# A hybrid decoder trunk: two pairs of column groups in each feed-forward stage become 2x2 block products with seven multiplications

## The chip, the core and the metric

One core of one Trainium2 chip runs the whole kernel in one launch. The metric is the device time of one execution in microseconds (us), lower is better. Before the change the three runs shown took 1042.58, 1043.15 and 1047.03 us, median 1043.15 us.

## What is computed

Two layers, and in each of them three stages on x of 256 tokens by 1024 channels, float32:

```
x += 1/2 * rmsnorm(swiglu(rmsnorm(x, g1)), post1)     # feed-forward stage 1
x +=       rmsnorm(hybrid_mix(rmsnorm(x, gm)), postm) # token mixing
x += 1/2 * rmsnorm(swiglu(rmsnorm(x, g2)), post2)     # feed-forward stage 2
swiglu(h) = (silu(h @ w_gate) * (h @ w_up)) @ w_down  # 1024 -> 2816 -> 1024
```

`hybrid_mix` projects to 2432 columns, runs four head groups side by side (a short gated convolution, a gated MLP over chunks, an RWKV-7 recurrence in chunk form, a convolution module) and projects back to 1024. The change touches the feed-forward stages; in the mixing it touches only how buffers are laid out.

## The kernel before, in words

The tokens are two tiles of 128 rows (b = 0, 1). A feed-forward stage walks through 11 column groups of 256 hidden channels. For a group i there are three weight blocks in memory: two for the gate and up columns side by side (1024 rows by 512 columns, in two row halves of 512 rows each) and one for the down projection. Each block is loaded as two tiles of 128 partitions x 1024 elements (512 KB), so a group has six loads.

`split` (line 124) makes one such load usable for TensorE. It loads the tile into one of four staging buffers (`raw`, line 127, issued on SyncE's queue), ScalarE rounds it to the float32r type (`whi`, line 135), and VectorE subtracts that from the staged tile (`wlo`, line 136). The tags `w` and `w2` give 14 and 10 buffers, so 12 pairs of parts exist at a time. `mm3` (lines 142 to 145) multiplies with three matmuls: high by high, high by low, low by high. The activations are split in the same way (`xh`, `xl`, lines 181 and 182).

`GU(b, i)` (line 243) is the gate/up product of one token tile with one group: 8 row blocks x 3 = 24 matmuls of 128x512 into one PSUM bank, then silu on ScalarE and the gating on VectorE; both read the bank and both scale by `r`, the norm's factor of each token. `TR(b, i)` (line 257) transposes the 256 gated channels on TensorE and splits the result (`hh`, `hl`). `DN(b, i)` (line 268) is the down product: 12 matmuls into two banks that accumulate over the whole stage. From group 2 on the loop (line 305) traces, for each group i: the loads and splits of group i, GU(0, i), TR(1, i-1), the loads of the down block i-1, DN(0, i-1), TR(0, i), GU(1, i), DN(1, i-1). That makes 24 + 12 + 24 + 12 = 72 matmuls of 128x512 and two calls of TR for each turn of the loop.

No order is written out by hand there. A scheduler that runs when the program is built walks through the traced instructions by priority, lets one go ahead of an earlier one when its operands and a free buffer are there by its own estimate of times, and so fixes the order of each engine's queue. On the chip each engine then takes its queue strictly in that order, and waits at the head when an operand is late. Calls marked `keep_in_program_order` or `later` are pinned.

PSUM has eight banks: four for the down sums (`acc`), two for products (`mm`) and two for transposes (`tp`). In SBUF the work pools are `c1` (10 buffers of 256 columns), `c2` (4 of 512), `f1` (8 of 256) and `f2` (4 of 512). The prenorm (lines 160 to 200) transposes x into `xg`, multiplies by the gain and splits it; `mix` (line 325) has its own single buffers for `lora`, `sgw`, `sgln`, `DC`, `caT`, `zc` and `pc0`, `pc1`.

Of the kernel before, what the change touches and what calls it, by code (L numbers as in the profile page):

```python
# [41 lines left out]
C1 = 10  # L42
# [6 lines left out]
def trunk_kernel(ctx: ExitStack, tc: tile.TileContext, a, out):  # L49
# [5 lines left out]
    act = ctx.enter_context(tc.tile_pool(name="act", bufs=1))  # L55
    work = ctx.enter_context(tc.tile_pool(name="work", bufs=2))
# [103 lines left out]
    def prenorm_steps(l, b, gname):  # L160
        xh = act.tile([P, KT, P], F32R, name=f"xh{b}")
        xl = act.tile([P, KT, P], F32R, name=f"xl{b}")
# [3 lines left out]
        def turn(h, pin=False):  # L166
# [6 lines left out]
            xg[h] = work.tile([P, 4, P], F32, name="xg", tag="f2", bufs=F2)  # L173
# [5 lines left out]
        def parts(h):  # L179
            sl = slice(4 * h, 4 * h + 4)  # L180
            nc.scalar.copy(xh[:, sl, :], xg[h])
            nc.vector.tensor_tensor(out=xl[:, sl, :], in0=xg[h], in1=xh.bitcast(F32)[:, sl, :], op=ALU.subtract)

        def stats():
# [6 lines left out]
            return xh, xl, r[:, 0:1]  # L191
# [3 lines left out]
    def prenorm(l, b, gname, pin=False):  # L195
        turn, parts, stats = prenorm_steps(l, b, gname)
# [25 lines left out]
    def ffn(l, f, nxt, first):  # L222
# [20 lines left out]
        def GU(b, i, middle=None):  # L243
            xh, xl, r = X[b]
            pg = mm_bank("pgu")
            for k in range(KT):
                hi, lo = gu[i][k // 2]
                mm3(pg, xh[:, k, :], xl[:, k, :], hi, lo, (k % 2) * 512, 512, k == 0, k == KT - 1)
# [35 lines left out]

        prep_gu(0)
# [19 lines left out]
        for i in range(2, NG):  # L305
            if first and i == 3:
                late_constants()
            prep_gu(i)
            GU(0, i)
            TR(1, i - 1)  # L310
            prep_dn(i - 1)
            DN(0, i - 1)
            TR(0, i)
            GU(1, i)
            if i == NG - 1:
# [3 lines left out]
            DN(1, i - 1)  # L319
# [5 lines left out]
    def mix(l, nxt):  # L325
        gp = load_gp(3 * l + 1)
        X = nxt["X"]
        lora = act.tile([P, 768], F32, name="lora")
        later(lora, a["lora"][l])
        sgw = act.tile([P, 4, P], F32, name="sgw")  # L330
        later(sgw, a["sgw"][l])
        sgln = act.tile([P, 512], F32, name="sgln")
# [35 lines left out]
        def proj(g, b):  # L368
            n = GROUPS[g][1]
            xh, xl, r = X[b]  # L370
            pairs, kp = W[g]
            pg = mm_bank("pin")
            for k in range(KT):
                hi, lo = pairs[k // kp]
                mm3(pg[:, 0:n], xh[:, k, :], xl[:, k, :], hi, lo, (k % kp) * n, n, k == 0, k == KT - 1)
# [9 lines left out]
        pc = [act.tile([P, 11, P + 1], F32, name=f"pc{b}") for b in range(NB)]  # L385
# [3 lines left out]
        def c_in(b):  # L389
            r = X[b][2]  # L390
# [11 lines left out]
        def c_prep(b):  # L402
# [45 lines left out]
            # kappa, its squared norm  # L448
# [20 lines left out]
            # chunk operands  # L469
# [20 lines left out]
            # v with tokens on partitions, bonus  # L490
# [39 lines left out]
        DC = act.tile([P, 8, 32], F32, name="DC")  # L530
# [6 lines left out]
        def c_base():  # L537
            # the inverse of every 16x16 diagonal block, even and odd columns on a partition each
# [75 lines left out]
        def own(bank):  # L614
            # of the four heads' regions, the columns that are the head's own
# [92 lines left out]
        zT = act.tile([P, 2, 256 + 30], F32, name="zT")  # L708
        nc.gpsimd.memset(zT[:, :, 0:30], 0.0)
        ca_T = act.tile([P, 2, 256 + 2], F32, name="caT")  # L710
# [9 lines left out]
        def d_in(b):  # L720
            pg = proj(2, b)
            r = X[b][2]
# [12 lines left out]
        zc = act.tile([P, 2, 256], F32, name="zc")  # L735
# [30 lines left out]
        def a_in(b):  # L766
            r = X[b][2]
# [10 lines left out]
        def a_out(b):  # L778
            r = X[b][2]
# [19 lines left out]
        def b_in(b):  # L799
            r = X[b][2]  # L800
# [94 lines left out]
    turn, parts, stats = prenorm_steps(0, 0, "g1")  # L895
# [12 lines left out]
    def third_step():  # L908
        cur["X"][1] = prenorm(0, 1, "g1", True)

    for n, (kind, l, f, _) in enumerate(phases):
        nx = {"X": [None, None]}
        if n + 1 < len(phases):
            nl, ng = phases[n + 1][1], phases[n + 1][3]

            def start(b, nl=nl, ng=ng, nx=nx):
                nx["X"][b] = prenorm(nl, b, ng)
# [127 lines left out]
```

## Time and profile before

| | |
|---|---|
| runs, median | 1042.58 to 1047.03, 1043.15 us |
| profiled execution, its span | 1043.0 us |
| TensorE matmul | busy 98% of the span |
| VectorE / ScalarE / GpSimd | 64% / 51% / 7% |
| bytes moved | 177 MB, 170 GB/s on average |

The profiled execution gives its span, from the first to the last instruction; no other time is known for it, and its 1043.0 us lie 0.15 us below the median of the runs. The busy time of TensorE counts matmuls whose ends are modelled, so that neighbours overlap: a matmul shown with 0.39 us starts about 0.23 us after the one before it. What a matmul costs is therefore read from the distance between two starts, not from its duration.

### The profile page before, as it was taken

Reading aid. Unit: us, or ns where it says so; the run is one execution under the profiler, and the core shown is the slowest. Engines: PE = TensorE matmul, PEld = TensorE weight load, DVE = VectorE, ACT = ScalarE, POOL = GpSimd, SP = SyncE. Lnnn points to the kernel's source line nnn. Section 1 sums busy time; section 2 is a strip of 40 time slices with the busy share of each in tenths; the row PEclk is TensorE's granted clock in tenths of the full one; section 3 lists DMA queues with packets and bytes.
Section 4 is the critical chain, followed back from the end, with each engine's and each line's share of the span. In section 5 each row is a group of like instructions: output and inputs, shape, how many; then the busy total and the mean of one; then the engine's idle time right before and its main releaser. Section 6 shows DMA issues by size and latency. Waiting matters only on the chain.

```text
span 1043.0 us, 13547 instructions
## 1 busy us (share of the span) xinstructions
PE 1018.7 (98%) x4914; PEld 834.5 (80%) x4914; DVE 669.7 (64%) x1072; ACT 533.7 (51%) x848; POOL 69.5 (7%) x133
## 2 busy tenths in 40 slices
PE   7999999999999999999999999999999999999997
PEld 6888888888797788888887888888878887888885
DVE  6754645689998655464676454647999895645442
ACT  6653534468466545353555353536665674535331
POOL 1000000210012100000010000003000130000000
PEclk8999999999999999999999999999999999999999
DMA  7865546254044654555536555544432356555521
GB/s 274 299 206 187 189 174 209 95 174 149 18 159 163 224 202 163 200 176 188 185 139 230 194 181 182 192 153 146 167 107 79 104 205 239 174 189 187 176 81 40
DMA packets 50322, 177.23 MB, mean 170 GB/s; under 512 B 5840, under 2 KB 6352, under 8 KB 50256
## 3 DMA queue, kind: packets, MB, share of 16 engines
q1 hardware_dynamic: 49968, 175.86, 49.9%
q8 instruction: 38, 0.62, 0.2%
q10 hardware_dynamic: 288, 0.52, 0.1%
q14 instruction: 28, 0.23, 0.1%
HBM read 175.31 MB, written 1.05 MB: 169 GB/s over the span
## 4 chain that ended last, share of the span: by engine, by line
PE 87%; DVE 7%; DMA 2%; POOL 1%; issue 1%; ACT 1%; SPq 0%; DVEq 0%; POOLq 0%; ACTq 0%
PE pgu L144 15%; PE pgu L143 15%; PE pgu L145 15%; PE dn L143 8%; PE dn L144 8%; PE dn L145 8%; PE pin L144 3%; PE pin L145 3%; PE pin L143 3%; DMA raw<-in_ffn 2%; PE hTp L261 2%; PE zp L586 1%; PE xT L170 1%; PE wo L143 1%; PE wo L144 1%
## 5 line engine op out<-in xcount | busy, mean ns | idle before, releaser
L136 DVE TENSOR_TENSOR wlo<-raw,whi 128x1024 fp32r<-128x1024 f32 x324 | 393.3, 1218 | 123.7 <-ACT whi L135 109.0
L135 ACT CAST whi<-raw 128x1024 fp32r<-128x1024 f32 x324 | 338.0, 1047 | 154.1 <-DMA raw<-in_ffn 63.4
L143 PE MATMUL pgu<-whi,xh 128*128 128x512 f32 x704 | 280.4, 398 | 4.0 <-ACT whi L135 4.0
L144 PE MATMUL pgu<-wlo,xh 128*128 128x512 f32 x704 | 276.7, 393 | 0.5 <-DVE wlo L136 0.5
L145 PE MATMUL pgu<-whi,xl 128*128 128x512 f32 x704 | 276.0, 392 | 0.0
L143 PEld LDWEIGHTS pgu<-whi,xh 128*128 128x128 f32 x704 | 132.8, 189 | 31.7 <-ACT whi L135 4.3
L145 PEld LDWEIGHTS pgu<-whi,xl 128*128 128x128 f32 x704 | 132.8, 189 | 28.9
L144 PEld LDWEIGHTS pgu<-wlo,xh 128*128 128x128 f32 x704 | 132.9, 189 | 27.4 <-DVE wlo L136 1.0
L143 PE MATMUL dn<-whi,hh 128*128 128x512 f32 x352 | 143.1, 406 | 3.6 <-ACT hh L264 3.6
L144 PE MATMUL dn<-wlo,hh 128*128 128x512 f32 x352 | 139.7, 397 | 0.0
L145 PE MATMUL dn<-whi,hl 128*128 128x512 f32 x352 | 138.1, 394 | 0.0
L252 ACT ACTIVATE silu<-pgu,rpre 128x256 f32<-128x256 f32 x88 | 41.5, 472 | 153.2 <-PE pgu L145 153.2
L254 DVE SCALAR_TENSOR_TENSOR h<-pgu,rpre,silu 128x256 f32<-128x256 f32 x88 | 42.3, 481 | 114.8 <-ACT silu L252 114.5
L265 DVE TENSOR_TENSOR hl<-hTp,hh 128x256 fp32r<-128x256 f32 x88 | 36.8, 418 | 91.2 <-ACT hh L264 91.2
L264 ACT CAST hh<-hTp 128x256 fp32r<-128x256 f32 x88 | 32.4, 368 | 99.1 <-PE hTp L261 99.0
L143 PEld LDWEIGHTS dn<-whi,hh 128*128 128x128 f32 x352 | 66.2, 188 | 19.1 <-ACT hh L264 4.9
L145 PEld LDWEIGHTS dn<-whi,hl 128*128 128x128 f32 x352 | 66.0, 188 | 16.9 <-DVE hl L265 1.0
L144 PEld LDWEIGHTS dn<-wlo,hh 128*128 128x128 f32 x352 | 66.2, 188 | 13.5
L144 PE MATMUL pin<-wlo,xh 128*128 128x512 f32 (+2 forms) x192 | 70.7, 371 | 0.0
L145 PE MATMUL pin<-whi,xl 128*128 128x512 f32 (+2 forms) x192 | 70.5, 371 | 0.0
L143 PE MATMUL pin<-whi,xh 128*128 128x512 f32 (+2 forms) x192 | 70.5, 371 | 0.0
L745 DVE SCALAR_TENSOR_TENSOR zc<-zT,par,zc 128x256 f32<-128x256 f32 x120 | 49.8, 477 | 3.2 <-ACT zc L742 3.1
(212 smaller groups left out, 908.4 us busy)
## 6 DMA issues: line engine op xcount, KB each, us to landing
raw<-in_ffn SPq DMA_DIRECT2D x264, 512.0 KB, 4.5
raw<-in_wout SPq DMA_DIRECT2D x16, 512.0 KB, 3.6
raw<-in_win_z SPq DMA_DIRECT2D x8, 512.0 KB, 4.5
raw<-in_win_rk SPq DMA_DIRECT2D x8, 512.0 KB, 5.0
raw<-in_win_ca SPq DMA_DIRECT2D x8, 512.0 KB, 4.3
raw<-in_win_uv SPq DMA_DIRECT2D x8, 512.0 KB, 4.5
gp<-in_post_g SPq DMA_DIRECT2D x6, 512.0 KB, 4.6
raw<-in_win_vl SPq DMA_DIRECT2D x8, 384.0 KB, 3.0
```

What stands on the lines that cost most here:

```text
L135: i0 = nc.scalar.copy(hi[:, 0:n], raw[:, 0:n])
L136: i1 = nc.vector.tensor_tensor(out=lo[:, 0:n], in0=raw[:, 0:n], in1=hi.bitcast(F32)[:, 0:n], op=ALU.subtract)
L143: nc.tensor.matmul(dst, lhsT=sh, rhs=hi[:, c0:c0 + n], start=start, stop=False)
L144: nc.tensor.matmul(dst, lhsT=sh, rhs=lo[:, c0:c0 + n], start=False, stop=False)
L145: nc.tensor.matmul(dst, lhsT=sl, rhs=hi[:, c0:c0 + n], start=False, stop=stop)
L170: t = nc.tensor.transpose(tp[:, k * P:(k + 1) * P], x[b][:, kk * P:(kk + 1) * P], ident)
L252: nc.scalar.activation(out=s, in_=pg[:, 0:256], func=AF.Silu, scale=r)
L254: nc.vector.scalar_tensor_tensor(out=h, in0=pg[:, 256:512], scalar=r, in1=s, op0=ALU.mult, op1=ALU.mult)
L261: nc.tensor.transpose(tp[:, j * P:(j + 1) * P], h[:, j * P:(j + 1) * P], ident)
L264: nc.scalar.copy(hh, tp[:, 0:256])
L265: nc.vector.tensor_tensor(out=hl, in0=tp[:, 0:256], in1=hh.bitcast(F32), op=ALU.subtract)
L745: nc.vector.scalar_tensor_tensor(out=zc[:, j, :], in0=zT[:, j, k:k + 256], scalar=w, in1=zc[:, j, :], op0=ALU.mult, op1=ALU.add)
```

## The change

In each feed-forward stage the groups (4, 5) and (7, 8) are taken as pairs. With the two token tiles as block rows and the two halves of the 1024 input channels as blocks of the inner dimension, a pair is a 2x2 by 2x2 block product; each block product is 12 matmuls. It is computed with seven block products (the Winograd form of Strassen's scheme) where eight stood. The signs are put on the token side, so that all sums of weight blocks are plain additions:

```
s1 = x10 - x11    s2 = s1 - x00    s3 = x00 - x10    s4 = x01 + s2
T1 = Bi0 + Bm0    T2 = T1 + Bm1    T3 = Bm0 + Bm1    T4 = T2 + Bi1
```

Here xbh is token tile b, channel half h, and Bgh the gate/up block of group g (i is the first of the pair, m the second), row half h. T1, T2 and T4 are made in place, one after the other, in the two tiles `chain`; T3 is made in two staging buffers. Each addition is a DMA issued from GpSimd that adds the tile in HBM to the tile in SBUF (`accum_op=ALU.add`). Each of the seven weight operands is split into high and low parts.

For these sums the token factor `r` has to be in the operands, not behind the product: after group 2 `scaled(b)` transposes `r` on TensorE and multiplies it into the kept `xg`, and `put` splits the result; groups from 3 on use these tiles (`A`). `forms()` makes s1 to s4. All such operands, the activations of the mixing and `lora`/`DC`, `sgw`/`sgln`, `caT`/`zc` share eight slots (`xsp`); `chain` shares the buffers of `pc`; `xg` of a feed-forward stage stays in the `c2` buffers; `c1` has 8 buffers for 10. The loop over groups carries a list of the groups whose down products are still open.

```diff
+PAIRS = (4, 7)
+SCALED = 3
-C1 = 10
+C1 = 8
...
+    xsp = ctx.enter_context(tc.tile_pool(name="xsp", bufs=8))
...
-    def split(src, shared, pin=False):
-        n = src.shape[-1]
+    def load(src):
         raw = rawp.tile([P, 1024], F32, name="raw", tag="raw")
-        nc.sync.dma_start(raw[:, 0:n], src)
+        nc.sync.dma_start(raw[:, 0:src.shape[-1]], src)
+        return raw
+
+    def parts_of(raw, n=1024, shared="mix", pin=False):
...
+    def split(src, shared, pin=False):
+        return parts_of(load(src), src.shape[-1], shared, pin)
...
         def GU(b, i, middle=None):
-            xh, xl, r = X[b]
             pg = mm_bank("pgu")
+            if i >= SCALED:
+                product(A[b], gu[i], pg, True, True)
+                gated(b, i, pg)
+                return
...
+        def product(t, pairs, bank, start, stop):
+            for kk in range(KT if len(t) == 2 else 4):
+                hi, lo = pairs[kk // 2]
+                f, k = t[kk // 4], kk % 4
...
+                for n, (m, w) in enumerate(((0, hi), (0, lo), (1, hi))):
+                    nc.tensor.matmul(bank, lhsT=f[:, m, k, :], rhs=w[:, c0:c0 + 512],
...
+        def put(v):
+            t = form_tile("form")
+            nc.scalar.copy(t[:, 0], v)
+            nc.vector.tensor_tensor(out=t[:, 1], in0=v, in1=t.bitcast(F32)[:, 0], op=ALU.subtract)
+            return t
+
+        def scaled(b):
+            _, r, xg = X[b]
+            tp = tp_bank("rT")
+            nc.tensor.transpose(tp[:, 0:P], r.broadcast_to([P, P]), ident)
+            for h in range(2):
+                nc.vector.tensor_tensor(out=xg[h], in0=xg[h], in1=tp[:, 0:P].unsqueeze(1).broadcast_to([P, 4, P]),
+                                        op=ALU.mult)
+            A[b] = [put(xg[h]) for h in range(2)]
+
+        def forms():
+            x00, x01, x10, x11 = (X[b][2][h] for b in range(2) for h in range(2))
...
+            s1 = sums(x10, x11, ALU.subtract)
+            form["s1"] = put(s1)
+            s2 = sums(s1, x00, ALU.subtract)
+            form["s2"] = put(s2)
+            form["s3"] = put(sums(x00, x10, ALU.subtract, x10))
+            form["s4"] = put(sums(x01, s2, ALU.add, x01))
+
+        def kept(bank, name):
+            t = work.tile([P, 512], F32, name=name, tag="f2", bufs=F2)
+            nc.scalar.copy(t, bank)
+            return t
+
+        def joined(b, i, p, q, op):
+            c = work.tile([P, 512], F32, name="c", tag="c2", bufs=C2)
+            nc.vector.tensor_tensor(out=c, in0=p, in1=q, op=op)
+            gated(b, i, c)
...
+        def two(i, m, prev):
...
+            def plus(p, g, t0):
+                for u in range(2):
+                    nc.gpsimd.dma_start(p[u], piece(g, t0 + u), accum_op=ALU.add)
+                return p
...
+            chain = [act.tile([P, 1024], F32, name=f"chain{u}", tag=f"pc{u}") for u in range(2)]
+            for u in range(2):
+                nc.sync.dma_start(chain[u], piece(i, u))
+            ba, bb, bc = mm_bank("pa"), mm_bank("pb"), tp_bank("pc")
+            product(A[0][0:1], both(chain), ba, True, True)
+            q1 = kept(ba, "q1")
+            plus(chain, m, 0)
+            for g in prev:
+                TR(1, g)
+            prep_dn(prev[-1])
+            for g in prev[:-1]:
+                DN(1, g)
+            DN(0, prev[-1])
+            product(A[0][1:2], both(fresh(i, 2)), bb, True, True)
+            joined(0, i, bb, q1, ALU.add)
+            DN(1, prev[-1])
+            product([form["s1"]], both(chain), bc, True, True)
+            p5 = kept(bc, "p5")
+            plus(chain, m, 2)
+            TR(0, i)
+            t3 = plus(fresh(m, 0), m, 2)
+            product([form["s2"]], both(chain), ba, False, True)
+            n2 = kept(ba, "n2")
+            plus(chain, i, 2)
+            prep_dn(i)
+            DN(0, i)
+            product([form["s3"]], both(t3), ba, False, True)
+            n3 = kept(ba, "n3")
+            joined(1, m, p5, n3, ALU.subtract)
+            product([form["s4"]], both(fresh(m, 2)), bc, False, True)
+            joined(0, m, bc, n2, ALU.subtract)
+            product(A[1][1:2], both(chain), ba, False, True)
+            gated(1, i, ba)
+            TR(0, m)
...
+            if i == 2:
+                scaled(1)
+                forms()
...
-        lora = act.tile([P, 768], F32, name="lora")
+        loraDC = mix_tile("loraDC", 1024)
+        lora = loraDC[:, 0:768]
```

Beside `product`, `gated` is silu and gating without `r`, `both` splits two tiles, `fresh` loads two tiles into staging buffers, and `piece(g, t)` names the t-th quarter of a group's gate/up block.

## Rows read from the trace of the kernel before

**Rows 1.** The page: busy time by engine; tenths in 40 slices; the chain by engine.
```profile
PE 1018.7 (98%) x4914; PEld 834.5 (80%) x4914; DVE 669.7 (64%) x1072; ACT 533.7 (51%) x848; POOL 69.5 (7%) x133
...
PE   7999999999999999999999999999999999999997
...
DVE  6754645689998655464676454647999895645442
ACT  6653534468466545353555353536665674535331
...
PEclk8999999999999999999999999999999999999999
DMA  7865546254044654555536555544432356555521
...
PE 87%; DVE 7%; DMA 2%; POOL 1%; issue 1%; ACT 1%; SPq 0%; DVEq 0%; POOLq 0%; ACTq 0%
```
**Rows 2.** Stretches: length, busy time (instructions) by engine, granted clock, DMA share, GB/s.
```profile
350.00:530.00 180.00, 177.35 (x796) 144.07 (x795) 101.97 (x117) 89.15 (x121) 3.87 (x6) 1.00 0.56 188
...
370.00:520.00 150.00, 150.00 (x673) 122.02 (x672) 79.43 (x90) 69.33 (x92) 0.00 (x0) 1.00 0.54 182
```
**Rows 3.** The chain in order of time, 350:530: start, length, what.
```profile
388.94 0.23 PE dn L143
...
405.93 0.24 PE dn L143
...
422.98 0.23 PE dn L143
```
**Rows 4.** TensorE's timeline, 418:423: start, length, line, out<-in.
```profile
417.80 0.39 PE L143 MATMUL pgu<-whi,xh 128*128 128x512 f32 x1
...
422.36 0.40 PE L145 MATMUL pgu<-whi,xl 128*128 128x512 f32 x1
```
**Rows 5.** Groups by line and shape: count | busy us, mean ns | idle before it.
```profile
L136 DVE TENSOR_TENSOR wlo<-raw,whi 128x1024 fp32r<-128x1024 f32 x316 | 385.1, 1223 | 122.5 <-ACT whi L135 108.2 <-PE u L640 0.5
L135 ACT CAST whi<-raw 128x1024 fp32r<-128x1024 f32 x316 | 331.3, 1052 | 146.4 <-DMA raw<-in_ffn 63.4 <-PE pgu L144 60.9 <-PE dn L144 12.8
...
L252 ACT ACTIVATE silu<-pgu,rpre 128x256 f32<-128x256 f32 x88 | 41.5, 472 | 153.2 <-PE pgu L145 153.2
L265 DVE TENSOR_TENSOR hl<-hTp,hh 128x256 fp32r<-128x256 f32 x88 | 36.8, 418 | 91.2 <-ACT hh L264 91.2
...
L264 ACT CAST hh<-hTp 128x256 fp32r<-128x256 f32 x88 | 32.4, 368 | 99.1 <-PE hTp L261 99.0
...
L182 DVE TENSOR_TENSOR xl<-xg,xh 128x512 fp32r<-128x512 f32 x24 | 15.9, 686 | 0.5 <-ACT xh L181 0.4
...
L181 ACT CAST xh<-xg 128x512 fp32r<-128x512 f32 x24 | 14.3, 617 | 11.2 <-DVE xg L174 11.1
...
L589 ACT COPY zz<-zp 128x512 f32<-128x512 f32 x12 | 7.0, 585 | 2.5 <-PE zp L586 2.5
```
**Rows 6.** DMA: an issue's KB and us to landing; landing of all staged loads.
```profile
raw<-in_ffn SPq DMA_DIRECT2D x264, 512.0 KB, 4.5
...
DMA to landing us min/median/max: 2.9/4.4/9.1
```
**Rows 7.** Waits of ScalarE and SyncE's queue, 370:520: us in total, times, longest.
```profile
ACT hh L264 <- PE hTp L261: 22.5, 9, 2.5
ACT whi L135 <- PE pgu L144: 15.5, 36, 0.8
ACT whi L135 <- DMA raw<-in_ffn: 11.5, 9, 1.8
...
SPq L127 <- DVE wlo L136: 127.9, 53, 8.9
```
**Rows 8.** Stretches of 10 us in the mixing stage, columns as in rows 2.
```profile
220.00:230.00 10.00, 10.00 (x51) 8.17 (x50) 10.00 (x23) 3.82 (x6) 0.00 (x0) 1.00 0.15 46
...
290.00:300.00 10.00, 10.00 (x84) 9.47 (x83) 9.95 (x26) 6.54 (x13) 1.01 (x2) 1.00 0.36 118
...
310.00:320.00 10.00, 8.98 (x59) 7.50 (x58) 7.76 (x31) 4.51 (x10) 4.28 (x6) 1.00 0.42 149
```

More of the change, by code (lines that the diff above doesn't have):

```diff
@@ L157, in rms, with form_tile, mix_tile, prenorm_steps @@
         return r
-    def prenorm_steps(l, b, gname):
-        xh = act.tile([P, KT, P], F32R, name=f"xh{b}")
-        xl = act.tile([P, KT, P], F32R, name=f"xl{b}")
+    def form_tile(name):
+        return xsp.tile([P, 2, 4, P], F32R, name=name, tag="xs", bufs=8)
+    def mix_tile(name, n):
+        return xsp.tile([P, n], F32, name=name, tag="xs", bufs=8)
+    def prenorm_steps(l, b, gname, keep):
+        xs = [form_tile("xs") for h in range(2)]
         g = col(l, gname, 0, 8)
@@ L172, in turn @@
                     tc.keep_in_program_order(t)
-            xg[h] = work.tile([P, 4, P], F32, name="xg", tag="f2", bufs=F2)
+            if keep:
+                xg[h] = work.tile([P, 4, P], F32, name="xg", tag="c2", bufs=C2)
+            else:
+                xg[h] = work.tile([P, 4, P], F32, name="xg", tag="f2", bufs=F2)
             v = nc.vector.tensor_tensor(out=xg[h], in0=tp.rearrange("p (k t) -> p k t", k=4),
@@ L179, in parts @@
         def parts(h):
-            sl = slice(4 * h, 4 * h + 4)
-            nc.scalar.copy(xh[:, sl, :], xg[h])
-            nc.vector.tensor_tensor(out=xl[:, sl, :], in0=xg[h], in1=xh.bitcast(F32)[:, sl, :], op=ALU.subtract)
+            nc.scalar.copy(xs[h][:, 0], xg[h])
+            nc.vector.tensor_tensor(out=xs[h][:, 1], in0=xg[h], in1=xs[h].bitcast(F32)[:, 0], op=ALU.subtract)
         def stats():
@@ L190, in stats, with prenorm @@
             r = rms(ss, RMS_EPS, "rpre")
-            return xh, xl, r[:, 0:1]
+            return xs, r[:, 0:1], xg
         return turn, parts, stats
-    def prenorm(l, b, gname, pin=False):
-        turn, parts, stats = prenorm_steps(l, b, gname)
+    def prenorm(l, b, gname, keep, pin=False):
+        turn, parts, stats = prenorm_steps(l, b, gname, keep)
         for h in range(2):
@@ new lines, in gated @@
+        def gated(b, i, c):
+            s = work.tile([P, 256], F32, name="silu", tag="f1", bufs=F1)
+            nc.scalar.activation(out=s, in_=c[:, 0:256], func=AF.Silu)
+            h = work.tile([P, 256], F32, name="h", tag="f1", bufs=F1)
+            nc.vector.tensor_tensor(out=h, in0=c[:, 256:512], in1=s, op=ALU.mult)
+            hs[b, i] = h
+        def put(v):
[3 more added lines that the diff above has]
+            return t
@@ new lines, in scaled, with sums @@
+        def scaled(b):
[8 more added lines that the diff above has]
+            x00, x01, x10, x11 = (X[b][2][h] for b in range(2) for h in range(2))
+            def sums(p, q, op, into=None):
+                t = into if into is not None else work.tile([P, 4, P], F32, name="sum", tag="f2", bufs=F2)
+                nc.vector.tensor_tensor(out=t, in0=p, in1=q, op=op)
+                return t
[5 more added lines that the diff above has]
+            form["s4"] = put(sums(x01, s2, ALU.add, x01))
@@ L304, in ffn @@
         gp = load_gp(3 * l + 2 * f)
-        for i in range(2, NG):
+        i = 2
+        prev = [1]
+        while i < NG:
             if first and i == 3:
                 late_constants()
+            if i in PAIRS:
+                two(i, i + 1, prev)
+                prev = [i, i + 1]
+                i += 2
+                continue
             prep_gu(i)
             GU(0, i)
-            TR(1, i - 1)
-            prep_dn(i - 1)
-            DN(0, i - 1)
+            if i == 2:
+                scaled(0)
+            for g in prev:
+                TR(1, g)
+            prep_dn(prev[-1])
+            for g in prev[:-1]:
+                DN(1, g)
+            DN(0, prev[-1])
             TR(0, i)
             GU(1, i)
+            if i == 2:
+                scaled(1)
+                forms()
             if i == NG - 1:
@@ L382, in c256 @@
             return work.tile([P, 256], F32, name=name, tag="c1", bufs=C1)
-        pc = [act.tile([P, 11, P + 1], F32, name=f"pc{b}") for b in range(NB)]
+        pc = [act.tile([P, 11, P + 1], F32, name=f"pc{b}", tag=f"pc{b}") for b in range(NB)]
         nc.gpsimd.memset(pc[0][:, 0:7, 0:1], 0.0)
@@ L893, in trunk_kernel @@
         phases += [("ffn", l, 0, "g1"), ("mix", l, 0, "gm"), ("ffn", l, 1, "g2")]
-    turn, parts, stats = prenorm_steps(0, 0, "g1")
+    turn, parts, stats = prenorm_steps(0, 0, "g1", True)
     turn(0)
```

55 lines of the change are left out of this document (37 added, 18 removed).

## The prediction

> **What bounds the kernel now.** I read the page first: TensorE's matmuls are busy for 98% of the span, its share of the chain that ended last is 87%, and the granted clock is full (2.4 GHz) in every slice but the first [rows 1]. A busy TensorE could still be one that waits inside, so the stretches came next: in a feed-forward stage, from 370 to 520 us, TensorE is busy 150.00 of 150.00 us while VectorE has 79.43 and ScalarE 69.33, and the 16 DMA engines a share of 0.54 [rows 2]. Then who runs ahead. In that stretch SyncE's queue stands waiting for `wlo` 53 times, and ScalarE's `whi` copies wait mostly for TensorE to let go of a buffer [rows 7]: the weights are early, and the buffers hold them back. So a feed-forward stage costs what its matmuls cost, and whatever takes matmuls out shows in full until another queue is late.
>
> **What one matmul costs.** From 417.80 to 422.36 there are 20 starts, 4.56 us, so 0.228 us each [rows 4]. One turn of the loop is 405.93 - 388.94 = 16.99 us, the next 17.05 [rows 3]; 72 matmuls take 16.42 of 17.0, so the two calls of TR take 0.29 us each, 0.15 for a transpose.
>
> **What is removed.** A pair was four GU calls, 96 matmuls; seven products are 84. Two pairs in four stages: 8 x 12 x 0.228 = 21.9 us, all of it on the path that sets the end.
>
> **What is added on TensorE.** `scaled` transposes `r` twice a stage: 8 x 0.15 = 1.2 us. Its other work and `forms` lie on VectorE and ScalarE: per stage 4 multiplications, 4 sums and 8 `put` subtractions of 512 columns at 0.686 us are 11.0 us of VectorE, and 8 copies at 0.617 are 4.9 us of ScalarE [rows 5]. They fall into group 2 and the first half of group 3. `A[0]` is due 5.8 + 5.5 us of TensorE work after GU(0, 2), and the s-forms two turns later; VectorE is 53% busy there, and 11 us more within some 30 us fit. I take nothing; if the cover were gone, the last `put` behind `A[1]` would cost about 2 us a stage, 8 us.
>
> **The pair on TensorE.** With t = 0 at the first product P1, in traced order: P1 to 2.7; TR, DN(0) to 5.8; P2 to 8.5; DN(1) to 11.2; P5 (T1) to 14.0; TR, P6 (T2) 14.3 to 17.0; DN to 19.7; P7 (T3) to 22.5; P3 to 25.2; P4 (T4) to 27.9; TR, 28.2 us in all (120 matmuls and 3 TR).
>
> **ScalarE and VectorE in the pair.** 18 tiles are split where 12 were, as each product needs its own two and the down blocks four. VectorE: 18 x 1.223 = 22.0, three `joined` sums at about 0.69, four gatings and four `hl` at 0.42: 27.4 us. ScalarE: 18 x 1.052 + four `kept` copies at 0.585 + four silu at 0.472 + four `hh` at 0.368 = 24.6 us [rows 5]. VectorE is thus 97% full for 28.2 us, against 53% around it [rows 2]. It holds because the 12 pairs of buffers let the splits lead by about half of that, and the single group after the pair (20 us of TensorE) asks only 9.4 us of VectorE, so the debt is paid back before the next pair. The cost is in answers that come a slot later: P7 may not write its bank before `kept` has read P6 (2.7 us of DN between), P4 not before P7 is read (2.7 us of P3 between), and the last TR needs three small operations after P3 (2.7 us between). In the queue ahead of such an answer stands at most one split, about 1.2 us. From below this is nothing; from above, each of the three late by one split, 3.7 us a pair, 29 us. I take 0.6 us a pair, 4.8 us, as the cover is longer than one split plus the operation in two of the three places.
>
> **The chain of weight sums.** This is the part that the trace does not show: there is no transfer issued by GpSimd in it, and none that adds. The work per pair is eight plain loads as before and eight adding ones. How late may one land? T1's first buffer comes free 6.8 us before t = 0 (GU(1, 3) gives back one pair of parts each 1.37 us from then on), so its second tile is split by -3.2 us, and only then may T2's addition go out, on GpSimd's queue, behind whose wait stand only further additions and, much later, the norm's small operations. With L the time to landing: T2 is there at -3.2 + L and due at 15.7, which allows L = 16. T4 goes out when T2 is split, 2.3 us and one split in the queue (1.2) after its landing, so it lands at 0.3 + 2L; its second half must be rounded by 26.6: 0.3 + 2L + 2.3 = 26.6, L = 12.0 us. T1 itself has some 13 us from the copy of Bi0 on, T3 more. So up to L = 12 the sums cost nothing; beyond it each us of L costs two a pair, 16 us in all.
>
> The bounds of L: a plain load of 512 KB lands in 2.9 to 9.1 us, median 4.4 [rows 6]; as an addition also has to fetch what it adds to, I put twice the longest, 18.2, as the upper end, and twice the median, 8.8, as my value, near the longest plain load. That is inside 12, so I take nothing here. At the ends: 0, and (18.2 - 12) x 16 = 99 us.
>
> The Trainium skill ("Collectives: The Full Stack", Part 3, on the fold count) says that an adding transfer runs at half of a copy's rate because it reads two sources through the same ring, with a measured ratio of 1.93. No run here shows it yet; by it an addition would fill the engines for an estimated 3.0 us, and the sum would come out near the first rival below, about 1060 us.
>
> **The mixing.** `c1` has 8 buffers for 10 in the stretch where VectorE is 100% busy and TensorE begins to show gaps (8.98 of 10 us) [rows 8]. At most ten of these tiles are asked for at a time, and the first to be given back is some operations of 0.4 us away. Nothing, or up to 4 us a layer; I take 0.5 us a layer. Sharing the slots changes when `lora` can be fetched, not what waits for it: two of the four slots from the forms are free 60 us before.
>
> **Sum.** 1043.0 (the profiled span, 0.15 us under the median of the runs) - 21.9 + 1.2 + 4.8 + 1.0 = 1028.1, so 1028 us. The floor, with all that is added hidden, is 1022.3.
>
> **Rivals.**
> *The adding transfers are too slow* (the other side). In the stretch from one pair to the next (28.2 + 20.0 = 48.2 us) there are 18 plain loads and 8 additions. A plain load fills all 16 engines for 1.56 us (0.56 of 180 us, at 188 GB/s 64.5 loads) [rows 2]. If an addition fills them as long, 26 x 1.56 = 40.6 us: it goes. If it fills them twice as long, 18 x 1.56 + 8 x 3.12 = 53.0 us, 4.8 us a pair too much, and L at that load is no longer 9 us: with L = 14, TensorE waits 4 us a pair for T4. 8 x 4 = 32 us over the forecast by the chain, 38 by the engines: about 1060 us, and it turns to a loss against 1043 at L of about 13. For it: eight additions go out in pairs, into a queue of engines that already has bursts. Against it: the share has 0.46 left, and chain and buffers lead. At L = 18 it would be above 1120.
>
> *The queues' fixed order.* The scheduler places the split of T2 and T4 by its own idea of when they land. If that is 3 us early, ScalarE stands at the head of its queue with `hh`, silu and `kept` behind it, and TensorE waits for them about 2.3 us a pair on top of my 0.6: 8 x 2.3 = 18 us, so 1046; half of it gives 1037. For it: ScalarE's waits for staged loads have that form already (9 waits, 11.5 us) [rows 7]. Against it: TensorE noticed none of them in that stretch [rows 2].
>
> *VectorE becomes the bound of the pair.* With four splits of the next group drawn into it, 22 x 1.22 + 5.5 = 32 us against 28.2: 3.8 us a pair if no lead is left, 30 us, no better than 1053; with half the lead left 1038. For it the 97%; against it, that the four are due only after the pair.
>
> **How the numbers follow.** Forecast 0.56 (its own range 1021 to 1038, faster throughout); slow transfers 0.23; fixed order 0.13, VectorE 0.08, both spread from 1036 to 1053. About 0.5% (5.2 us) is what a measurement can tell from no change. Faster by more than that: 0.56 and a fifth of the last two, 0.60. Within: over half of the last two, 0.13. Slower: the slow transfers with the rest, 0.27. The range runs from 1020, under the floor by the error of the cadence, to 1064; above lies the slow transfer from L = 14.3 on, about 0.13, and below 0.03.
>
> **What would show it.** Right: 96 matmuls fewer, cadence still 0.228 us, granted clock full, no row of TensorE waiting for a split of `chain` or for `kept`, additions landing under 12 us. The first rival: landing of 13 us or more, DMA share near 1 in the pairs, TensorE waiting for `whi` there, and the clock dropping after such waits. The second: ScalarE waiting for an adding transfer while `hh` or silu is overdue. The third: VectorE full, `wlo` the releaser of TensorE. The forecast is wrong if a stage isn't about 4 us shorter than its 11 turns of 17.0 us.

## The result and the profile after

The change makes the kernel slower: 1107.38 us (median of 4, 1104.26 to 1111.77) against 1043.34 us for the kernel before beside it, a ratio of 1.0602, 95% interval 1.0576 to 1.0629. The forecast was 1028 us in a range of 1020 to 1064, so both the sign and the range were wrong. The profiled execution took 1111.77 us, its span is 1110.1.

The page of the changed kernel, the lines that answer to [rows 1], with the line of the adding DMAs' queue (packets, MB, share of 16 engines' span):

```profile
PE 1032.4 (93%) x4826; PEld 828.5 (75%) x4826; DVE 766.3 (69%) x1208; ACT 602.4 (54%) x960; POOL 116.8 (11%) x197
...
PEclk9998989999999998999999989899999999989899
...
q0 software_dynamic: 9216, 33.56, 16.8%
...
PE 55%; DMA 22%; DVE 12%; issue 5%; ACT 4%; POOL 1%; SPq 0%; POOLq 0%; DVEq 0%; ACTq 0%
```

TensorE has fewer instructions, as meant, but it is no longer the bound: its part of the chain falls from 87% to 55%, DMA's rises from 2% to 22%, and the clock has dips that were not there. TensorE's waits (total us, times, longest):

```profile
PE hTp L281 <- DVE h L324: 43.3, 8, 6.3
PE dn L151 <- ACT hh L284: 9.6, 8, 3.0
```

Eight times, once for each pair, a transpose of TR waits for `h`: 5.4 us on average. All of TensorE's waits together are 70.4 us; before they were 17.7. ScalarE's longest sum of waits, and the DMA issues (KB, us to landing), to be held against [rows 7] and [rows 6]:

```profile
ACT whi L140 <- DMA chain<-in_ffn: 84.4, 27, 7.2
```
```profile
raw<-in_ffn SPq DMA_DIRECT2D x248, 512.0 KB, 4.8
chain<-in_ffn POOLq DMA_DIRECT2D x48, 512.0 KB, 8.0
```

One pair shows how these hang together. It is the second of the first stage; its P1 starts at 140.92. ScalarE's timeline (start, length, what, [idle before <- what ended it]):

```profile
153.04 1.05 ACT L140 CAST whi<-raw 128x1024 fp32r<-128x1024 f32 x1 [2.36 <-DMA raw<-in_ffn]
156.81 1.04 ACT L140 CAST whi<-chain 128x1024 fp32r<-128x1024 f32 x1 [2.72 <-DMA chain<-in_ffn]
157.76 1.04 ACT L140 CAST whi<-raw 128x1024 fp32r<-128x1024 f32 x1
158.71 0.41 ACT L322 ACTIVATE silu<-c 128x256 f32<-128x256 f32 x1
159.02 1.03 ACT L140 CAST whi<-chain 128x1024 fp32r<-128x1024 f32 x1
```

VectorE, GpSimd and TensorE around it, and between them the chain of what released what, followed back from 162:

```profile
155.26 0.68 DVE L365 TENSOR_TENSOR c<-pb,q 128x512 f32<-128x512 f32 x1
157.89 1.23 DVE L141 TENSOR_TENSOR wlo<-chain,whi 128x1024 fp32r<-128x1024 f32 x1 [1.94 <-ACT whi L140]
159.03 1.22 DVE L141 TENSOR_TENSOR wlo<-raw,whi 128x1024 fp32r<-128x1024 f32 x1
160.16 0.42 DVE L324 TENSOR_TENSOR h<-c,silu 128x256 f32<-128x256 f32 x1
```
```profile
148.63 0.87 POOL L377 DMA_DIRECT2D chain<-in_ffn  x1 [1.60 <-DVE wlo L141]
```
```profile
139.77 6.24 DMA chain<-in_ffn
...
148.63 8.10 DMA chain<-in_ffn
...
156.81 1.05 ACT whi L140
```
```profile
154.86 0.40 PE L316 MATMUL pc<-whi,form 128*128 128x512 f32 x1
160.73 0.66 PE L281 MATMUL hTp<-ident,h 128*128 128x128 f32 x2 [5.47 <-DVE h L324]
161.04 0.77 PE L316 MATMUL pa<-whi,form 128*128 128x512 f32 x1
...
165.04 0.39 PE L316 MATMUL pa<-whi,form 128*128 128x512 f32 x1
```

T4 is made by two additions, one for each of its tiles. The second of them goes out at 148.63 and lands 8.10 us later, and the first split of T4 starts at that moment, 156.81. (The first one went out at 146.16 and had landed at 151.9; by the trace's semaphores its tile is split last, at 159.02, and so it is in all eight pairs. The other order was not tried.) T4 is the operand of the last product of the pair, due 25 us after P1, at about 166. But its split stands in ScalarE's queue ahead of silu of the first joined group, whose transpose is due when P5 ends, 14 us after P1. So silu waits for a transfer that it does not need, `h` waits for silu behind two `wlo`, and TensorE stands still for 5.47 us.

T4's addition is not the only late transfer there. On either side of its first split stand the splits of `fm` (`fresh(m, 2)`, the two plain loads for P3, which is due after that transpose too). The first kept ScalarE waiting for 2.36 us before 153.04, and its `wlo` stands ahead of `c` on VectorE, which so starts at 155.26. The second went out at 149.50, 0.87 us behind T4's addition, and landed at 156.94, 0.2 us after it: 7.4 us for a plain load. All eight pairs show this: that load takes 6.9 to 8.2 us and lands 0.2 to 0.4 us after the addition; with copies in place of the additions (e3 below) it takes 4.8 to 5.6. So the additions come late and slow the plain loads beside them, and silu stands behind three late splits; T4 alone in time would have let the last of them start some 0.8 us sooner (156.94 for 157.76), an estimate.

The next product, P6, takes 4.23 us (161.04 to 165.27) where twelve matmuls take 2.74, because the granted clock has fallen (columns as in [rows 2]):

```profile
150.00:160.00 10.00, 5.26 (x23) 3.91 (x22) 6.06 (x6) 4.91 (x7) 0.00 (x0) 0.86 1.00 324
160.00:170.00 10.00, 9.27 (x35) 7.54 (x36) 6.78 (x8) 5.84 (x9) 0.11 (x1) 0.80 0.75 247
```

Over all stretches of 10 us, ten times the missing share of the clock sums to 32.8 us, against 5.9 before. The mixing stages are as long as before (82.8 to 82.9 us from the first input product to the first output product in both), so the shared slots and the 8 buffers of `c1` cost nothing there.

### The profile page after: what moved, and what is told of

Same layout as the page of the kernel before. It is cut to its first block, busy times and chain, and to the rows that moved or that the text cites. A ratio compares the mean times of both kernels' runs of the same rounds, so it can differ in the third digit from the quotient of the medians.

```text
span 1110.1 us, 13796 instructions
## 1 busy us (share of the span) xinstructions
PE 1032.4 (93%) x4826; PEld 828.5 (75%) x4826; DVE 766.3 (69%) x1208; ACT 602.4 (54%) x960; POOL 116.8 (11%) x197
## 3 DMA queue, kind: packets, MB, share of 16 engines
q0 software_dynamic: 9216, 33.56, 16.8%
## 4 chain that ended last, share of the span: by engine, by line
PE 55%; DMA 22%; DVE 12%; issue 5%; ACT 4%; POOL 1%; SPq 0%; POOLq 0%; DVEq 0%; ACTq 0%
DMA chain<-in_ffn 15%; PE pgu L316 10%; DMA raw<-in_ffn 7%; PE pa L316 6%; PE dn L151 4%; DVE wlo L141 4%; PE dn L153 4%; PE dn L152 4%; ACT whi L140 4%; PE pin L152 3%; PE pin L153 3%; PE pin L151 3%; PE pgu L151 2%; PE pgu L152 2%; PE pgu L153 2%
## 5 line engine op out<-in xcount | busy, mean ns | idle before, releaser
L141 DVE TENSOR_TENSOR wlo<-raw,whi 128x1024 fp32r<-128x1024 f32 (+1 forms) x308 | 372.0, 1217 | 113.3 <-ACT whi L140 107.3
L140 ACT CAST whi<-raw 128x1024 fp32r<-128x1024 f32 (+1 forms) x308 | 319.2, 1044 | 148.4 <-DMA raw<-in_ffn 45.1
L316 PE MATMUL pgu<-whi,form 128*128 128x512 f32 x512 | 168.1, 398 | 0.0
L141 DVE TENSOR_TENSOR wlo<-chain,whi 128x1024 fp32r<-128x1024 f32 x64 | 78.1, 1223 | 97.6 <-ACT whi L140 96.8
L316 PEld LDWEIGHTS pgu<-whi,form 128*128 128x128 f32 x512 | 95.9, 188 | 21.3
L316 PE MATMUL pgu<-wlo,form 128*128 128x512 f32 x256 | 100.8, 394 | 0.0
L316 PE MATMUL pa<-whi,form 128*128 128x512 f32 x256 | 97.4, 444 | 0.0
L151 PE MATMUL pgu<-whi,xs 128*128 128x512 f32 x192 | 78.6, 410 | 2.1 <-ACT whi L140 2.0
L152 PE MATMUL pgu<-wlo,xs 128*128 128x512 f32 x192 | 77.9, 406 | 1.2 <-DVE wlo L141 1.2
L153 PE MATMUL pgu<-whi,xs 128*128 128x512 f32 x192 | 77.0, 402 | 0.6 <-DVE xs L197 0.6
L151 PE MATMUL pin<-whi,xs 128*128 128x512 f32 (+2 forms) x192 | 70.9, 373 | 0.0
L153 PE MATMUL pin<-whi,xs 128*128 128x512 f32 (+2 forms) x192 | 70.9, 372 | 0.0
```

Of the source, the lines that this page charges most:

```text
L151: nc.tensor.matmul(dst, lhsT=sh, rhs=hi[:, c0:c0 + n], start=start, stop=False)
L152: nc.tensor.matmul(dst, lhsT=sh, rhs=lo[:, c0:c0 + n], start=False, stop=False)
L153: nc.tensor.matmul(dst, lhsT=sl, rhs=hi[:, c0:c0 + n], start=False, stop=stop)
L316: nc.tensor.matmul(bank, lhsT=f[:, m, k, :], rhs=w[:, c0:c0 + 512], start=start and kk == 0 and n == 0, stop=last and n == 2, skip_group_c ...
```

## Experiments

Each ratio is to the kernel before on the same chip (medians there 1043.68 to 1044.55 us). In the diffs `...` stands for what is left out.

**e1: the last splits behind silu and h.** `issue_after` queues an instruction behind another on its engine.

```diff
-            joined(0, i, bb, q1, ALU.add)
+            first_h = joined(0, i, bb, q1, ALU.add)
...
-            product([form["s4"]], both(fresh(m, 2)), bc, False, True)
+            product([form["s4"]], both(fresh(m, 2), first_h), bc, False, True)
...
-            product(A[1][1:2], both(chain), ba, False, True)
+            product(A[1][1:2], both(chain, first_h), ba, False, True)
```

> The splits of the P3 and P4 operands (fm and T4) are queued on ScalarE and VectorE behind the silu and the gating of the pair's first output; nothing else is changed. Theory A (the fixed queue order: ScalarE stands at the head with T4's split, whose addition has not landed, and the silu that TR(0, i) needs is behind it): the eight waits of TR for h (43 us) and the half-speed matmuls after them (some 2.4 us each, 19 us) go, so 1107 - 62 = 1045 us, between 1035 and 1055, with the additions landing as late as before (about 8 us). Theory B (the adding transfers are too slow for the chain, or fill the engines): the wait only moves from TR to P4 or P6, over 1085 us. Theory C (VectorE and ScalarE have too much to do in a pair): the order cannot help, over 1085 us, with VectorE near 100% in the pairs.

1090.74 us, ratio 1.0447 (1.0414 to 1.048): 17 us back, where 52 or more were expected. The wait for `h` went (3.9 us), but the same splits, those of `fm` and T4, now hold up the next small operation, `hh` of that transpose:

```profile
PE dn L151 <- ACT hh L284: 30.4, 15, 4.6
```

**e2: e1, and T2's and T3's splits behind hh and hl of TR(1, prev).**

```diff
+                last_t = TR(1, g)
...
+            product([form["s2"]], both(chain, last_t), ba, False, True)
...
+            product([form["s3"]], both(t3, last_t), ba, False, True)
```

> As the run before it, and the splits of T2 and T3 are queued behind hh and hl of the group that precedes the pair. Theory A: the waits of DN for hh (9.6 us) go too with what clock they cost, 5 to 12 us less than that run, 1030 to 1045 us. Theories B and C: no gain over it.

1078.43 us, 1.0327 (1.0301 to 1.0354): 12 us more are back. TensorE still waits for `hh` 10 times, 25.0 us. The longest eight of these waits come some 20 us after P1, at the `hh` of TR(0, i), still behind the splits of `fm` and T4.

**e3: GpSimd's DMAs copy and don't add.** The weight sums are left out; every engine's queue has the order of the changed kernel.

```diff
-                    nc.gpsimd.dma_start(p[u], piece(g, t0 + u), accum_op=ALU.add)
+                    nc.gpsimd.dma_start(p[u], piece(g, t0 + u))
```

> The additions from GpSimd's queue are plain copies (the weight sums are left out), with the same order of instructions in every queue. Theory A: a copy lands some 3 us earlier than an addition, twice along the chain, so T4's split comes 6 us earlier and the wait of TR (5.4 us) is about gone: 1040 to 1060 us. Theory B: the same or less, as the engines are freed: under 1045 us. Theory C: no change, over 1090 us.

1042.66 us, 0.9987 (0.9972 to 1.0001). So the additions are worth 1.0602 - 0.9987 = 0.0615, 64 us: the whole loss. In this kernel the same rows read:

```profile
q0 software_dynamic: 9216, 33.56, 9.6%
...
chain<-in_ffn POOLq DMA_DIRECT2D x48, 512.0 KB, 4.5
```
```profile
138.23 1.05 ACT L140 CAST whi<-chain 128x1024 fp32r<-128x1024 f32 x1 [0.35 <-PE pb L316]
140.06 1.05 ACT L140 CAST whi<-raw 128x1024 fp32r<-128x1024 f32 x1 [0.79 <-DMA raw<-in_ffn]
141.03 0.41 ACT L322 ACTIVATE silu<-c 128x256 f32<-128x256 f32 x1
```

Same pair, same queue; P1 starts at 129.73. The split of T4 finds its tile there, silu runs 11.3 us after P1 (17.8 in the changed kernel), and the transpose is in time. The fixed order fits a landing of 4.5 us and not one of 8. (A copy also keeps the DMA engines busy for less time, and its issue is shorter; this run doesn't tell these from the landing. That the order matters is shown by e1, e2 and e5, which change the order alone.)

**e4: no pairs.** Scaling, forms and shared slots stay.

```diff
-PAIRS = (4, 7)
+PAIRS = ()
```

> No pair is formed; the token factors in the operands, the forms, the shared slots and the smaller buffers all stay. What the rest of the change costs by itself: by my prediction 1.2 us of transposes and 1 us in the mixing, so 1043 + 2 = 1045 us; by a rival for which the extra 11 us of VectorE a stage or the fewer buffers matter, 1052 us or more. Under theory A the loss of 64 us belongs to the pairs and is not here.

1053.11 us, 1.0082 (1.0059 to 1.0105), 9 us more than before. No wait explains it (16.4 us in all): the matmuls themselves start further apart:

```profile
418.13 0.39 PE L316 MATMUL pgu<-whi,form 128*128 128x512 f32 x1
...
421.87 0.40 PE L316 MATMUL pgu<-wlo,form 128*128 128x512 f32 x1
```

Between the two rows lie 16 steps: 3.74 / 16 = 0.234 us, against 0.228 in [rows 4].

**e5: each waiting split behind hh and hl.** e2, with the splits of `fresh(m, 2)` (`fm`) and T4 behind hh and hl of TR(0, i).

```diff
-            product(A[1][1:2], both(chain, first_h), ba, False, True)
+            product(A[1][1:2], both(chain, first_t), ba, False, True)
```

> The changed kernel with every split of a pair that waits for an adding DMA queued behind the hh and hl copies of the transposes that come before it in TensorE's order: T2 and T3 behind those of TR(1, prev), the splits of fm and T4 behind those of TR(0, i). Nothing is left out. Theory A (what is lost is TensorE waiting for hh and h behind splits that wait for landings, and the cold clock after it): the waits of dn for hh (25.0 us in e2) and of hTp for h fall under 6 us together, as with plain copies, the granted clock is 0.99 or more, and the time is 1041 to 1050, close to the 1042.66 of e3. Theory B (the chain of split, addition of 8 us and split is too long for the pair wherever its splits stand): the waits come back at pa and pc, over 15 us in sum, for whi or wlo of the chain, and the time is 1058 to 1080.

1065.65 us, 1.0188 (1.0137 to 1.0239), between the two theories. The waits for `hh` are 3.2 us, but `h` is late again, 17.3 us in 10 waits, on VectorE this time: in the second pair T2's second half went out at 127.60 and lands 13.9 us later, where the median landing is 8.2, and its `wlo` with two plain ones stands ahead of `c`:

```profile
142.57 1.22 DVE L141 TENSOR_TENSOR wlo<-chain,whi 128x1024 fp32r<-128x1024 f32 x1 [1.89 <-ACT whi L140]
143.71 2.35 DVE L141 TENSOR_TENSOR wlo<-raw,whi 128x1024 fp32r<-128x1024 f32 x2
145.99 0.68 DVE L367 TENSOR_TENSOR c<-pb,q 128x512 f32<-128x512 f32 x1
```

Five of the ten waits come at this place, 15 to 18 us after P1; the longest of the others come some 32 us after P1 and were not followed.

**e6: the kernel before, its stationary tiles moved.** Only the addresses of `xh` and `xl` change.

```diff
+        act.tile([P, 352 if b == 0 else 8], F32, name=f"gapa{b}")
         xh = act.tile([P, KT, P], F32R, name=f"xh{b}")
+        act.tile([P, 8], F32, name=f"gapb{b}")
         xl = act.tile([P, KT, P], F32R, name=f"xl{b}")
```

> The kernel before with nothing changed but the addresses of its stationary operand: empty gaps before xh and xl put them 1056, 1088, 1120 ... bytes into a multiple of 4096, as the first shared slots of the changed kernel are (before, xh, xl, whi and wlo all start 3744 bytes into one). Theory A (the matmul starts of the products 0.232 us apart in e4 in place of 0.228 come from where the stationary tiles lie): pgu starts 0.231 to 0.233 apart and the time is 1049 to 1054. Theory B (the distance has another cause, as the different order of the loads or the added work on the other engines): 0.228 apart and 1042 to 1045.

1049.2 us, 1.0048 (1.0034 to 1.0062), and 20 steps take 4.67 us, 0.2335 each:

```profile
417.19 0.39 PE L143 MATMUL pgu<-whi,xh 128*128 128x512 f32 x1
...
421.86 0.39 PE L145 MATMUL pgu<-whi,xl 128*128 128x512 f32 x1
```

**e7: e5 with slots 4096 bytes apart.**

```diff
-C1 = 8
+C1 = 7
...
-        cz = mix_tile("cz", 1028)
-        ca_T = cz[:, 512:1028].rearrange("p (j t) -> p j t", j=2)
+        cz = mix_tile("cz", 512)
+        ca_T = act.tile([P, 2, 256 + 2], F32, name="caT")
```

> e5 with the shared slots exactly 4096 bytes apart and starting where whi and wlo start within a multiple of 4096 (the conv tile's 516 columns in a tile of its own, the pool ahead of the activations, C1 at 7 in place of 8 to pay for it, the two constant tiles of ones and bones in one place). Nothing is left out. Theory A (addresses): 7 to 10 us less than e5, so 1032 to 1042, the starts 0.228 apart. Theory B: as e5 within 2 us, or slower by what C1 at 7 costs the mixing.

1065.1 us, 1.0196 (1.0148 to 1.0244): as e5. The starts are 0.228 apart as expected, but a faster TensorE only waits longer (`h` 24.4 us for 17.3). What it gains is seen where nothing waits, in e10.

**e8: e7, sums on GpSimd.** A plain load into `raw` and an addition.

```diff
-                    nc.gpsimd.dma_start(p[u], piece(g, t0 + u), accum_op=ALU.add)
+                    r = load(piece(g, t0 + u))
+                    nc.gpsimd.tensor_tensor(out=p[u], in0=p[u], in1=r, op=ALU.add)
```

> e7 with every weight sum made by a plain load into a raw slot (512 KB, some 4.5 us) and a GpSimd addition of 128x1024, in place of the adding DMA of some 8 us. Nothing is left out. The addition's price is not in any trace here; a GpSimd memset of that shape took 0.95 us, and I take 1 to 4 us. Theory A (the landing of the adding DMA is the root): the time is e7's or up to 6 us less, 1027 to 1040, and the 16.8% of the DMA engines' time in the adding queue is halved. Theory B (four raw slots are too few for 8 more loads in each pair, SP's queue stops behind them, and whi of the plain tiles comes late): 1045 to 1075, with waits of pb, pgu and dn for whi.

1104.93 us, 1.0576 (1.0539 to 1.0613), worse than both theories.

```profile
L385 POOL TENSOR_TENSOR chain<-chain,raw 128x1024 f32<-128x1024 f32 x48 | 128.2, 2677 | 354.6 <-DVE wlo L143 281.8 <-DMA raw<-in_ffn 47.7 <-DVE h L327 25.1
```
```profile
L143 DVE TENSOR_TENSOR wlo<-chain,whi 128x1024 fp32r<-128x1024 f32 x64 | 114.5, 1799 | 17.2 <-ACT whi L142 16.4
```

An addition takes 2.68 us, and `wlo` of the sums, 1.22 in the other kernels, takes 1.80. TensorE waits 26.3 us for `hh` and 20.6 for `h`.

**e9: e7, each split behind what is due sooner.** `copies` holds the `kept` copies; the slices are n2 and n3.

```diff
+            product([form["s2"]], both(chain, first_h), ba, False, True)
+            product([form["s3"]], both(t3, first_t), ba, False, True)
+            product([form["s4"]], both(fresh(m, 2), copies[-2:-1]), bc, False, True)
+            product(A[1][1:2], both(chain, copies[-1:]), ba, False, True)
```

> e7 with each waiting split queued behind what TensorE needs sooner: the splits of the second sum (P6) behind silu and h of the first joined group (due 10.3 us into the pair, where the split is due 14.3), those of T3 behind hh and hl of TR(0, i), those of fm behind n2, those of T4 behind n3. Nothing is left out. Theory A (order alone: in e7 c and h of that group stood behind the second sum's splits, which land 10.7 to 12.5 us after their issue): the waits of hTp for h fall from 24.4 to under 8 us, the clock to 0.99, and the time is 1034 to 1046. Theory B (the landings under load are simply too late for P6, P7 or P4): the same waits come back at pa for whi or wlo, and the time stays 1055 to 1068.

1067.16 us, 1.023 (1.0197 to 1.0263). `h` is in time (2.9 us) and the clock is 0.996, but now the splits are late, and TensorE waits for VectorE's `wlo` in several products (45.0 us of waits in all):

```profile
PE pa L319 <- DVE wlo L143: 6.6, 15, 0.8
PE dn L153 <- ACT hh L286: 6.6, 6, 2.1
PE dn L154 <- DVE wlo L143: 4.3, 7, 0.8
PE pc L319 <- DVE wlo L143: 3.9, 7, 0.8
```

**e10: e4 with slots 4096 bytes apart.**

```diff
-PAIRS = (4, 7)
+PAIRS = ()
-C1 = 8
+C1 = 7
...
-        cz = mix_tile("cz", 1028)
+        cz = mix_tile("cz", 512)
```

> e4 (no pairs, the scaling, the forms and the shared slots in place) with the slots 4096 bytes apart as in e7, C1 at 7. Theory A (the 9 us of e4 are the addresses of the stationary tiles): 1042 to 1047, pgu starts 0.228 apart. Theory B (they are the scaling, the forms and the shared slots themselves): 1050 to 1055.

1047.95 us, 1.0045 (1.0028 to 1.0062). Again 16 steps, 3.67 / 16 = 0.229 us:

```profile
418.56 0.40 PE L318 MATMUL pgu<-whi,form 128*128 128x512 f32 x1
...
422.23 0.39 PE L318 MATMUL pgu<-wlo,form 128*128 128x512 f32 x1
```

e6, which changes nothing but addresses, shows that where the stationary tiles lie costs the kernel before 4 to 5 us; e10 against e4 agrees (3.9 us), though C1 is another there. Just over half of e4's 8.6 us remain; the scaling and C1 at 7 are in them, in parts not told apart.

**e11: sums on VectorE.** Slots and C1 as in e7, no split pinned: the scheduler's own order ("planner" in the expectations).

```diff
-                    nc.gpsimd.dma_start(p[u], piece(g, t0 + u), accum_op=ALU.add)
+                    r = load(piece(g, t0 + u))
+                    nc.vector.tensor_tensor(out=p[u], in0=p[u], in1=r, op=ALU.add)
```

> The changed kernel with every weight sum made by a plain load into a raw slot and a VectorE addition of 128x1024, slots 4096 bytes apart and C1 at 7 as in e7, the queues in the planner's own order. Nothing is left out. An addition should take what wlo takes, 1.22 us, so 64 of them add 78 us to VectorE's 766. Theory A (the landing of the adding DMA, some 8 us and up to 12.5, is the root, and the loads ahead of a VectorE addition can be early): the granted clock is 0.99 or more, TensorE's waits under 30 us in sum (70 in the changed kernel, 18 before), 1032 to 1045. Theory B (the sums cost the pair its time whoever makes them: 8 more loads through four raw slots, and VectorE late): waits over 40 us, 1050 to 1080, with dn, pa, pb or pgu waiting for whi or wlo of raw tiles.

1052.39 us, 1.0079 (1.0055 to 1.0103), between the two theories. An addition costs what was worked out, `h` and `hh` are late by 15.6 us in 15 waits, TensorE's waits are 37.3 us in all and the clock is 0.999. It is the best kernel here that makes the sums, and still slower than before.

```profile
L380 DVE TENSOR_TENSOR chain<-chain,raw 128x1024 f32<-128x1024 f32 x48 | 57.8, 1219 | 18.1 <-DMA raw<-in_ffn 18.0
```

**e12: e3 with slots 4096 bytes apart** (the sums are left out).

```diff
-                    nc.gpsimd.dma_start(p[u], piece(g, t0 + u), accum_op=ALU.add)
+                    nc.gpsimd.dma_start(p[u], piece(g, t0 + u))
...
-        cz = mix_tile("cz", 1028)
+        cz = mix_tile("cz", 512)
```

> e3 (GpSimd's DMAs copy and don't add, so the weight sums are left out; every queue as in the changed kernel) with the slots 4096 bytes apart and C1 at 7: what is left of the change when neither the landing of the additions nor the stationary tiles' addresses cost anything. Theory A: 7 to 9 us under e3 and 10 to 14 under e10, so 1032 to 1037. Theory B (the addresses matter less once TensorE waits here and there): 1039 to 1043.

1040.69 us, 0.9967 (0.9948 to 0.9986), nearer theory B. Against e10 the pairs now give 0.0078, 8 us, of the 21.9 that 96 matmuls are.

**e13: e9 with copies** (the sums are left out).

```diff
-                    nc.gpsimd.dma_start(p[u], piece(g, t0 + u), accum_op=ALU.add)
+                    nc.gpsimd.dma_start(p[u], piece(g, t0 + u))
```

> e9 with GpSimd's DMAs copying in place of adding (the weight sums are left out), every queue in e9's order. Theory A (what e9 still loses is the landing of the additions: TensorE then runs at the pace of splits that start when a sum has landed): waits for wlo gone, 1038 to 1044, as e12. Theory B (e9's order itself puts splits so late that TensorE waits for VectorE whatever lands when): 1055 to 1068, with the same waits of pa, pc and dn for wlo.

1044.94 us, 1.0008 (0.9993 to 1.0023). With e9's order the additions still cost 0.022, 23 us (TensorE's waits are 27.1 us for e9's 45.0): what this order did not bring back comes with the additions, not with the order. The landing of the chain's tiles is 5.7 us here and 8.4 in e9.

**e14: two copies for each addition** (the sums are left out).

```diff
-                for u in range(2):
-                    nc.gpsimd.dma_start(p[u], piece(g, t0 + u), accum_op=ALU.add)
+                for again in range(2):
+                    for u in range(2):
+                        nc.gpsimd.dma_start(p[u], piece(g, t0 + u))
```

> The changed kernel with each addition replaced by the same plain copy issued twice, the second after the first has landed (the weight sums are left out): about the time to landing and the engines' time of an addition, without adding; the planner sees both transfers and may place the splits later. Theory A (the landing and where the queues place it are the cause, not the adding as such): two landings of 4.5 to 5 us make 9 to 10, and the loss is back in part: 1055 to 1100. Theory B (the adding does harm of its own, to the other loads or to SBUF): as e3, 1040 to 1048.

1133.01 us, 1.083 (1.0792 to 1.0868), above theory A's range and far from B's: tiles that come late can do this without any adding. The run doesn't isolate the landing, as the scheduler placed the queues anew. That it is worse than the additions fits GpSimd's queue, where the second copy of a tile waits at the head for the first, with other tiles' copies behind it (91.9 us of such waits for `chain`, none in e3).

```profile
PE dn L151 <- ACT hh L284: 52.7, 14, 7.4
```

## Why the prediction was wrong, point by point

- *What is removed* was right in count (4914 TensorE instructions became 4826: 96 fewer matmuls, 8 transposes more).
- *0.228 us each* did not hold: 0.234 with the operands in the shared slots. Not foreseen; e6, and e10 against e4, put it at 4 to 5 us in a kernel without pairs.
- *Scaling and forms at nothing*: e10 has 4.7 us over before (2.9 to 6.5), with the 1.2 us of the transposes and about 1.5 us of longer mixing stages, where C1 is 7, inside. Nearly right.
- *The mixing* at 1.0 us: nothing measured with C1 at 8. One reading behind it was wrong: in [rows 8] VectorE is full in the two stretches where TensorE is too, and in the one with TensorE's gap (8.98) it has 7.76.
- *VectorE 97% full in the pair* counts four `hl` and four `hh`, where a pair has three TR; without the fourth it is 27.0 us, 96%. Nothing hangs on it.
- *Late answers at 0.6 us a pair*: even with copies e12 is 8 us under e10 and not 21.9, so 14 us are gone, 1.7 a pair (the upper bound given was 3.7). TensorE's named waits account for 6.5 of them (24.6 us against 18.1), which is 0.8 a pair; that the other half is late answers too is not shown.
- *The time to landing* was right: 8.8 us taken, 8.0 measured, 8.1 for T4 in the pair above. The latency chain, T4 there at 0.3 + 2L, gives 16.3 with L = 8; it was there 15.8 us after P1. That they are so near is in part luck: T2's second addition went out 1.2 us before P1 (139.77) and not 3.2, and landed in 6.24 us and not 8.
- *"Up to L = 12 the sums cost nothing"* is the step that failed. The chain was followed only to the product that uses T4, due 25 us after P1. The queues have another tolerance: the split of T4, and with it those of `fm`, stood ahead of a silu whose answer was due 11 us earlier. And *"in the queue ahead of such an answer stands at most one split"* counted a split as 1.2 us of work, not as a wait for a transfer. With it the additions cost 64 us at L = 8.
- *The queues' fixed order*, the second rival, named this mechanism, at 2.3 us a pair. The additions took 64 / 8 = 8 us a pair: the wait for `h` is 5.4 us on average, and the cold clock after it costs 1.5 us in the product looked at. The rest was not followed pair by pair. Reordering alone (e1, e2, e5) brought back 43 of the 64 us; that much is shown to be the order, as the additions stayed.
- *The adding transfers are too slow*, the first rival, had its place at T4 and its turn at L = 13; the median landing stayed below, yet the loss came. Its engines' side is visible: the share of DMA is 1.00 in the stretch from 150 to 160. With the queues put otherwise (e5, e7, e9) the times, 1065 to 1067, are near this rival's 1060, and e13 shows that what is left goes with the additions. The plain loads felt it too, which the chain left out: the one behind T4's addition took 6.9 to 8.2 us. And single additions went far past the median, 13.9 us in the pair of e5 shown.
- *VectorE the bound*: not in the changed kernel; in e9, where the splits start late, it is.

Left open: how e9's 23 us divide between the time from issue to landing and the engines' greater load, as no run changes one without the other.

## What to carry to other kernels

A transfer that an engine waits for must be in time not for its own consumer but for whatever stands behind that wait in the same queue; give each wait the due time of the earliest operation behind it. The same order was harmless here at a landing of 4.5 us and cost 6% at 8. When one wait is moved away, look for the next small operation behind it before counting the gain: three rounds of reordering brought back 43 of 64 us, a fourth (e9) nothing beyond that, and the saving in matmuls was never large enough to pay for the rest.

## What the runs showed of the hardware

- A DMA that adds fills the engines longer than one that copies: 16.8% of 1110.1 us against 9.6% of 1040.4 for the same 33.56 MB, 1.87 times, and its issue took GpSimd 0.87 us against 0.54. The Trainium skill ("Collectives: The Full Stack", Part 3) gives a measured ratio of 1.93 between the copying and the adding step of ring collectives; the 1.87 of this case's traces is near it. The median landing was 8.0 us (5.3 to 12.1) against 4.5 (3.4 to 7.0). A plain load of 512 KB issued 0.87 us behind an adding one landed after 6.9 to 8.2 us (eight cases), and after 4.8 to 5.6 behind a copy (e3).
- The distance of matmul starts depends on where the stationary tile lies in SBUF: in the stretches of gate and up products shown, 0.228 to 0.229 us where it starts at the same offset within 4096 bytes as the moving tiles, 0.234 where it starts elsewhere ([rows 4], e4, e6, e10). The offsets are those that e6's and e7's texts give, as no trace shows an address; which part of the address does it was not tried.
- A GpSimd addition of 128x1024 took 2.68 us, and `wlo` on VectorE beside it grew from 1.22 to 1.80 us (e8); the same addition on VectorE took 1.22 (e11).
